# Decode products in the banks of o, their turns two parts later, and the last normaliser stored as rows

## The chip, the core and the metric

The kernel runs on one core of a Trainium2 chip. A core has one TensorE (PE in the profile; its weight loads are PEld), VectorE (DVE), ScalarE (ACT), GpSimd (POOL) and SyncE (SP), each with an instruction stream of its own; they meet at semaphores. Transfers are issued by SP, GpSimd or ScalarE and carried by 16 DMA engines. TensorE writes its results to PSUM, which has 8 banks of 128 x 512 numbers in fp32. The metric is the device time in microseconds (us) of one execution, median over several.

## The reference

One inference step of a decoder trunk of one layer, for a new sequence of 1024 tokens and for 8 sequences with one new (decode) token each, all in fp32, width 1024:

```python
def hybrid_layer(x, h0, conv0, C0, n0, m0, ...):
    hn = rmsnorm(x, g_norm)
    u = hn @ w_in                                   # 1024 -> 7176
    xa, za, uq, uk, uv, uo, zb, ui, uf = jnp.split(u, SPLIT_IDX, axis=-1)
    yA, hA, bufA = rglru_branch(xa, conv0, h0, ...) # conv of 4, gates in 16 blocks, h = a*h + u
    q, k, v = ...                                   # 4 heads of 256
    hB, C, n, m = mlstm_seq(q, k, v, ig, lf, C0, n0, m0)   # 8 chunks of 128 tokens
    yB = ...                                        # sigmoid(uo) * hB, normalised per head
    merged = jnp.concatenate([yA * silu(za), yB * silu(zb)], axis=-1)
    x = x + merged @ w_out                          # 2048 -> 1024
    return x, hA, bufA, C, n, m

def mlstm_chunk(carry, inp):
    ...
    C_new = carry_scale[..., None, None] * C + jnp.einsum('bhs,bshk,bshv->bhkv', decay, k, v)
    n_new = carry_scale[..., None] * n + jnp.einsum('bhs,bshk->bhk', decay, k)
```

The outputs are both y, and the last states of both kinds of sequences; among them is the normaliser p_n of the long sequence, 4 heads of 256 numbers.

## The kernel before

**Products.** A product of fp32 matrices is three matmuls on split operands (`mm3`, L66 to L68): each operand is rounded to a shorter type (hi, a ScalarE cast, L72) and the rest is kept as a second operand (lo, a VectorE subtraction, L73). The input projection is cut into 14 units, counted from 0 (`UNITS`: "v0v1", "x0y0", "q0k0" and so on); a unit is 512 columns of `w_in`, two groups of 256. Each unit is computed by seven block products in place of eight (Q_P1, Q_P2, Q_P5, Q_P6, Q_P7, Q_P3, Q_P4, in this order), with combinations of the weight blocks that VectorE makes (L282, L284 and L290, 128x1024 each). `product` runs a block product in two halves; a half is called a part, some 3 us of TensorE, and after each part the main loop calls `pop_bg`, which puts steps of the other stages (gates, scans, decode, the mLSTM states) between the parts.

**PSUM banks.** They are handed out by tag: o has 3 banks, kv has 2, and tr, s and qp have one each. A product's X (Q_P1, Q_P6, Q_P7, Q_P4) is in kv and its Y (Q_P2 of its own; Q_P5 and then Q_P3 on top of it) in o: four o banks per unit, given out in turn. ScalarE or VectorE reads each bank out (`evac`), and its next user waits for that reader.

**The decode burst.** The 8 decode tokens need the same weights, before VectorE combines them. So `prep(u, Q_P5)`, which makes the operands two products ahead and so runs just before `product(u, Q_P1)`, first calls `dec_unit(u)`: eight matmuls into four groups of rows of one bank tr (L256, 16 rows in the trace since each fp32 matmul counts twice), a ScalarE copy of it to Z (L259), and `turn()`: four transposes of Z (L264) into a bank tr and two VectorE reduces (L267) that add the four groups and write them to the decode operands (dqk, dxz, do, dz). `turn` is put on the list `late`, which the next `pop_bg` runs first: one part later, after the first half of Q_P1. The one bank tr is also used by the RG-LRU gates (L824, every second half) and, in later stages, by `m_b` and the decode outputs.

**The end.** The mLSTM stage goes over 8 chunks and 4 heads (`m_a` to `m_z`). In the last chunk `m_b` stores each head's matrix state (L1260) and its normaliser, which lies as a column 256 of the state with one number per partition (L1261: four stores of 128x2x1 on GpSimd's queue). After that come the last chunk's outputs (`m_n`, `m_zg`, `m_z`), the output projection of the last two tiles (`out_part`, then `last_tile` in three column ranges) and the final norm. Staging tiles (`sg`, tag stg) come from 7 buffers that are given out in turn.

**Order.** The program is built in the order in which the functions are called; from that order, and from which banks and buffers are free, the scheduler of the framework fixes each engine's instruction stream when the program is built. An engine works through its stream in order.

Of the kernel before, what the change touches and what calls it, by code (L numbers as in the profile page):

```python
# [9 lines left out]
F32 = mybir.dt.float32  # L10
# [7 lines left out]
P = 128  # L18
T = 1024
HT = 512  # L20
NB = 8
KC = 8
NH = 4
# [28 lines left out]
def hymba_kernel(  # L52
# [7 lines left out]
    V, A, G, TE = nc.vector, nc.scalar, nc.gpsimd, nc.tensor  # L60
    ld = nc.sync.dma_start
    stq = nc.gpsimd.dma_start

    def mm3(out, ah, al, bh, bl, first, last):

        TE.matmul(out, ah, bh, start=first, stop=False, skip_group_check=True)  # L66
        TE.matmul(out, ah, bl, start=False, stop=False, skip_group_check=True)  # L67
        TE.matmul(out, al, bh, start=False, stop=last, skip_group_check=True)  # L68

    def split(hi, lo, src):  # L70

        a = A.copy(hi, src)  # L72
        V.tensor_tensor(lo, src, hi.bitcast(F32), op=ALU.subtract)  # L73
        return a
# [7 lines left out]
    def ps(tag, shape):  # L82
        return psp.tile(shape, F32, tag=tag, name=f"ps_{tag}", bufs=NBUF.get(tag, 1))

    def const(shape, name, dt=F32):
        return cpool.tile(shape, dt, tag=name, name=name)
# [14 lines left out]
    def sg(shape, name, dt=F32):  # L101

        return stg.tile(shape, dt, tag="stg", name=name)
# [9 lines left out]
    idF = const([P, P], "idF")  # L113
# [77 lines left out]
    def rsqrt_log(out, v, t):  # L191

        A.activation(t, v, AF.Ln, scale=2.0 ** 32)
        A.activation(out, t, AF.Exp, scale=-0.5)
        if len(v.shape) == 2 and v.shape[1] == 1:
            V.scalar_tensor_tensor(t, out, out, v, op0=ALU.mult, op1=ALU.mult)
        else:
            V.tensor_tensor(t, out, out, op=ALU.mult)
            V.tensor_tensor(t, t, v, op=ALU.mult)
        V.tensor_scalar(t, t, -0.25 * 2.0 ** 32, 0.75, op0=ALU.mult, op1=ALU.add)  # L200
        V.scalar_tensor_tensor(out, out, 2.0 ** 16, t, op0=ALU.mult, op1=ALU.mult)
# [18 lines left out]
    late = []  # L220
# [29 lines left out]

    def dec_unit(u):

        pz = ps("tr", [P, 512])
        for k in range(KC):
            g = k % 4
            TE.matmul(pz[32 * g:32 * g + 32, :], hnd[:, NB * k:NB * k + 32], raws[u, k // 4][:, k % 4, :], start=k < 4, stop=k >= 4,  # L256
                      skip_group_check=True)
        Z = sg([P, 512], "Z")
        A.copy(Z, pz)  # L259

        def turn():
            pt = ps("tr", [P, 4, P])
            for m in range(4):
                TE.transpose(pt[:, m, :], Z[:, m * P:(m + 1) * P], idF)  # L264
            for a, (kind, j) in enumerate(units[u]):
                src = pt[:, 2 * a:2 * a + 2].rearrange("p m (g b) -> p m b g", g=4)[:, :, 0:NB, :]
                V.tensor_reduce(dec_dst[kind](j), src, axis=mybir.AxisListType.X, op=ALU.add)  # L267
                if kind == "k":
                    V.tensor_scalar(dec_dst[kind](j), dec_dst[kind](j), 1.0 / 16.0, None, op0=ALU.mult)
        late.append(turn)  # L270


    wops = {}
# [307 lines left out]
    V.tensor_tensor(gd, pgd[0:NB], bgate[0:NB], op=ALU.add)  # L581
    ld(d_gd, gd)
    dec_unit(0)
    load_raw(1, 0)
    load_raw(1, 1)
# [514 lines left out]
    mx = {}  # L1100
# [109 lines left out]
    def m_kv(n, tags):  # L1210

        d, kvs = it[n], []
        for kb, tag in enumerate(tags):
            kv = ps(tag, [P, 258])
            mm3(kv, d["kh"][:, kb * P:(kb + 1) * P], d["kl"][:, kb * P:(kb + 1) * P], *mx["v"], True, True)
            kvs.append(kv)
        return kvs
# [26 lines left out]
    def m_b(n):  # L1244
        c, h = n // 4, n % 4
        d = it[n]
        qc = ps("qp", [P, 258])
        for kb in range(2):
            mm3(qc, d["qh"][:, kb, :], d["ql"][:, kb, :], d["Ch"][:, kb, :], d["Cl"][:, kb, :], kb == 0, kb == 1)
        d["hh"] = hh = mx["p"].tile([P, 257], F32, tag="hh", name="hh", bufs=5)  # L1250
        A.mul(hh, qc[:, 0:257], gi_t[:, c, h:h + 1])
        kvs = m_kv(n, ("kv", "kv"))
        pv = ps("tr", [P, 258])
        mm3(pv, d["ph"], d["pl"], *mx["v"], True, True)
        for kb in range(2):
            V.scalar_tensor_tensor(mx["Cf"][h][:, kb, :], mx["Cf"][h][:, kb, :], cs_b[:, c, h:h + 1], kvs[kb],
                                   op0=ALU.mult, op1=ALU.add)
        V.tensor_tensor(hh, pv[:, 0:257], hh, op=ALU.add)
        if c == NCH - 1:
            stq(p_C[0, 0, h].rearrange("(kb p) v -> p kb v", p=P), mx["Cf"][h][:, :, 0:256])  # L1260
            stq(p_n[0, 0, h].rearrange("(kb p o) -> p kb o", p=P, o=1), mx["Cf"][h][:, :, 256:257])  # L1261

    def m_g(n):

# [22 lines left out]
    def m_zg(c):  # L1287

        x = ch[c]
        for h in range(NH):  # L1290
            A.mul(x["g"][h], x["g"][h], x["m"][:, 3, h:h + 1])

    def m_z(c, pair):

        x = ch[c]
        ht = ps(("s", "qp")[pair], [P, 4, P])
        for i in range(2):
            g = x["g"][2 * pair + i]
            for vb in range(2):
                TE.transpose(ht[:, 2 * i + vb, :], g[:, vb * P:(vb + 1) * P], idF)  # L1300
        s = slice(4 * pair, 4 * pair + 4)
        z = zt[c][:, s, :]
        V.tensor_tensor(z, ht, z, op=ALU.mult)
        if c < NZ:
            stq(d_mz[c][pair], z)
            return
        if pair == 0:
            m_ops(c)
        split(x["mh"][:, s, :], x["ml"][:, s, :], z)

    def m_ops(c):

        ch[c]["mh"], ch[c]["ml"] = ws([P, 8, P], f"mh{c}"), ws([P, 8, P], f"ml{c}")
# [269 lines left out]

    LP = [slice(0, 512), slice(512, 768), slice(768, 1024)]

    def last_tile():
        ms = mx["p2"].tile([P, 6], F32, tag="ms7", name="ms7")
        y = [sg([P, HT], f"y{n}") for n in range(2)]
        yg = [sg([P, HT], f"yg{n}") for n in range(2)]
        for n in range(2):  # L1590
            ld(y[n], d_p[NCH - 1][n])
        mh, ml = ch[NCH - 1]["mh"], ch[NCH - 1]["ml"]
        for i, cs in enumerate(LP):
            p = ps("o", [P, 512])[:, 0:cs.stop - cs.start]
            for k in range(8):
                w = wo[8 + k]
                mm3(p, mh[:, k, :], ml[:, k, :], w[:, 0, cs], w[:, 1, cs], k == 0, k == 7)
            v = (y[0], y[1][:, 0:256], y[1][:, 256:512])[i]
            vg = (yg[0], yg[1][:, 0:256], yg[1][:, 256:512])[i]
            gv = (mx["gf"][0], mx["gf"][1][:, 0:256], mx["gf"][1][:, 256:512])[i]  # L1600
            V.tensor_tensor(v, v, p, op=ALU.add)
            A.activation(p, v, AF.Square, accum_out=ms[:, i:i + 1])
            V.tensor_tensor(vg, v, gv, op=ALU.mult)
            if i == 1:
                V.tensor_scalar(ms[:, 0:1], ms[:, 0:1], ms[:, 1:2], T * EPS, op0=ALU.add, op1=ALU.add)
        V.tensor_scalar(ms[:, 0:1], ms[:, 0:1], ms[:, 2:3], 0.25 / T, op0=ALU.add, op1=ALU.mult)
        rsqrt_log(ms[:, 4:5], ms[:, 0:1], ms[:, 5:6])
        V.tensor_scalar(yg[0], yg[0], ms[:, 4:5], None, op0=ALU.mult)
        A.mul(yg[1], yg[1], ms[:, 4:5])
        for n in range(2):  # L1610
            ld(y_p[0, (NCH - 1) * P:T, n * HT:(n + 1) * HT], yg[n])
# [3 lines left out]
    def fill(k):  # L1615
        for _ in range(k):
            while work:
                if next(work[0], work) is work:
                    work.popleft()
                else:  # L1620
                    break
# [90 lines left out]
    for n in range(4, N):  # L1712
        c, h = n // 4, n % 4
# [13 lines left out]
        if h == 0:  # L1727
            m_n(c - 1)
            fill(2 if n < N2 else 1)
            m_k(n + 1)  # L1730
            fill(1)
            m_b(n)
            fill(1)
        elif h == 1:
# [25 lines left out]
    m_n(last)  # L1760
    fill(3)
    m_zg(last)
    m_z(last, 0)
    fill(1)
    m_z(last, 1)
    while work:
        fill(1)
    tail()
    last_tile()
    es_m.close()  # L1770

# [32 lines left out]
```

## Time and profile before

| | |
|---|---|
| median of 3 runs | 918.35 us (917.04 to 923.15) |
| the profiled execution | 919.27 us, of it 917.2 in the span of the profile |
| TensorE (PE) busy | 902.7 us, 98% of the span |
| its weight loads (PEld) | 749.1 us, 82% |
| VectorE (DVE) | 740.8 us, 81% |
| ScalarE (ACT) | 590.1 us, 64% |
| GpSimd (POOL) | 195.5 us, 21% |
| mean DMA rate | 183 GB/s |

Busy time adds up the instructions of an engine, register and DMA-issuing instructions left out. A row of a timeline gives start (us from the span's start), duration, engine, operation, line, out<-in, sizes, and in brackets how long the engine had stood before it and what released it. The projection units run from about 80 to 625 us, the mLSTM stage to about 890 us, and the rest is the end.

### The profile page before, as it was taken

To read this page: it belongs to the slowest core of one execution; us is meant where nothing else is said; L and a number is where in the kernel's file an instruction comes from. 1 tells how busy PE (TensorE), PEld (TensorE's weight loads), DVE (VectorE), ACT (ScalarE), POOL (GpSimd) and SP (SyncE) were. 2 spreads that over 40 slices of the span, in tenths; PEclk is the share of its full clock that TensorE was granted. 3 is DMA by queue.
4 is the path that set the end of the run, shared out by engine and by line. 5 is a ranking of instruction groups with operands and counts; after the bars stand their busy time and mean duration, and the time that the engine had idled before them with its cause. 6 is when DMAs were issued, how large, how long until landed. Compare 5 with 4: busy or idle time off the path is not lost.

```text
span 917.2 us, 15521 instructions
## 1 busy us (share of the span) xinstructions
PE 902.7 (98%) x5257; PEld 749.1 (82%) x5257; DVE 740.8 (81%) x1532; ACT 590.1 (64%) x1085; POOL 195.5 (21%) x321
## 2 busy tenths in 40 slices
PE   8999999999999999999999999999999999999996
PEld 6897777877777988787779898877778888888886
DVE  6874778978698978789978876679998779889873
ACT  7663456867567676576758686446786568566642
POOL 1111113112312232324332434010111110121120
PEclk9999999999999999999999999999999999999999
DMA  6611457365646566647665747345679889856653
GB/s 201 193 62 45 138 173 243 132 197 188 220 132 208 172 196 205 202 144 256 199 211 193 275 138 243 101 138 185 194 226 280 198 204 302 228 135 182 186 102 88
DMA packets 130584, 167.68 MB, mean 183 GB/s; under 512 B 17700, under 2 KB 98660, under 8 KB 130498
## 3 DMA queue, kind: packets, MB, share of 16 engines
q1 hardware_dynamic: 108790, 103.68, 37.7%
q0 software_dynamic: 21712, 63.02, 21.4%
q8 instruction: 41, 0.67, 0.3%
q14 instruction: 37, 0.30, 0.1%
q10 hardware_dynamic: 4, 0.00, 0.0%
HBM read 108.00 MB, written 62.92 MB: 186 GB/s over the span
## 4 chain that ended last, share of the span: by engine, by line
PE 88%; DVE 4%; ACT 4%; DMA 3%; issue 1%; POOL 0%; ACTq 0%; DVEq 0%; POOLq 0%
PE ps_o L66 14%; PE ps_o L68 14%; PE ps_o L67 14%; PE ps_kv L66 10%; PE ps_kv L67 10%; PE ps_kv L68 10%; PE ps_tr L256 3%; PE ps_s L1195 1%; DMA Cb<-in_state_mlstm_C_dram 1%; DMA W<-d_alpha 1%; PE ps_qp L1013 1%; PE ps_qp L67 1%; PE ps_s L824 1%; PE ps_tr L264 1%; PE ps_qp L68 1%
## 5 line engine op out<-in xcount | busy, mean ns | idle before, releaser
L72 ACT CAST wh<-raw 128x1024 fp32r<-128x1024 f32 x91 | 95.3, 1048 | 73.8 <-PE ps_o L67 24.2
L73 DVE TENSOR_TENSOR wl<-raw,wh 128x1024 fp32r<-128x1024 f32 x91 | 111.0, 1220 | 34.3 <-ACT wh L72 18.8
L66 PE MATMUL ps_kv<-cb_hi,wh 128*128 128x512 f32 x320 | 127.5, 398 | 0.0
L68 PE MATMUL ps_kv<-cb_hi,wl 128*128 128x512 f32 x320 | 125.3, 392 | 0.0
L67 PE MATMUL ps_kv<-cb_lo,wh 128*128 128x512 f32 x320 | 125.2, 391 | 0.0
L66 PE MATMUL ps_o<-cb_hi,wh 128*128 128x512 f32 x240 | 94.7, 395 | 0.0
L68 PE MATMUL ps_o<-cb_hi,wl 128*128 128x512 f32 x240 | 93.7, 390 | 0.0
L67 PE MATMUL ps_o<-cb_lo,wh 128*128 128x512 f32 x240 | 93.5, 390 | 0.0
L66 PEld LDWEIGHTS ps_kv<-cb_hi,wh 128*128 128x128 f32 x320 | 60.1, 188 | 21.3 <-issue 5.5
L67 PEld LDWEIGHTS ps_kv<-cb_lo,wh 128*128 128x128 f32 x320 | 60.2, 188 | 13.4 <-issue 1.7
L68 PEld LDWEIGHTS ps_kv<-cb_hi,wl 128*128 128x128 f32 x320 | 60.1, 188 | 12.9
L66 PE MATMUL ps_kv<-wh,cb_hi 128*128 128x256 f32 x192 | 55.2, 287 | 0.0
L67 PE MATMUL ps_kv<-wl,cb_hi 128*128 128x256 f32 x192 | 54.4, 283 | 0.0
L68 PE MATMUL ps_kv<-wh,cb_lo 128*128 128x256 f32 x192 | 54.3, 283 | 0.0
L66 PEld LDWEIGHTS ps_o<-cb_hi,wh 128*128 128x128 f32 x240 | 45.1, 188 | 10.2 <-issue 0.8
L66 PE MATMUL ps_o<-wo,mh 128*128 128x512 f32 (+1 forms) x136 | 53.1, 390 | 0.0
L68 PEld LDWEIGHTS ps_o<-cb_hi,wl 128*128 128x128 f32 x240 | 45.0, 188 | 9.8
L67 PEld LDWEIGHTS ps_o<-cb_lo,wh 128*128 128x128 f32 x240 | 45.1, 188 | 9.1
L68 PE MATMUL ps_o<-wo,ml 128*128 128x512 f32 (+1 forms) x136 | 51.7, 380 | 0.0
L67 PE MATMUL ps_o<-wo,mh 128*128 128x512 f32 (+1 forms) x136 | 51.5, 379 | 0.0
L66 PE MATMUL ps_o<-wh,cb_hi 128*128 128x256 f32 x144 | 40.9, 284 | 0.0
L67 PE MATMUL ps_o<-wl,cb_hi 128*128 128x256 f32 x144 | 40.7, 283 | 0.0
(547 smaller groups left out, 2600.7 us busy)
## 6 DMA issues: line engine op xcount, KB each, us to landing
raw<-in_w_in_dram SPq DMA_DIRECT2D x55, 512.0 KB
Cb<-in_state_mlstm_C_dram SPq DMA_DIRECT2D x32, 256.0 KB
out_dram<-Cb POOLq DMA_DIRECT2D x32, 256.0 KB, 4.4
qk<-d_qk SPq DMA_DIRECT2D x32, 256.0 KB
ring<-d_ro SPq DMA_DIRECT2D x28, 256.0 KB
d_qk<-s POOLq DMA_DIRECT2D x24, 256.0 KB, 4.5
d_x<-s POOLq DMA_DIRECT2D x16, 256.0 KB, 3.1
zsr<-d_y SPq DMA_DIRECT2D x16, 256.0 KB
```

Of the source, the lines that this page charges most:

```text
L66: TE.matmul(out, ah, bh, start=first, stop=False, skip_group_check=True)
L67: TE.matmul(out, ah, bl, start=False, stop=False, skip_group_check=True)
L68: TE.matmul(out, al, bh, start=False, stop=last, skip_group_check=True)
L72: a = A.copy(hi, src)
L73: V.tensor_tensor(lo, src, hi.bitcast(F32), op=ALU.subtract)
L256: TE.matmul(pz[32 * g:32 * g + 32, :], hnd[:, NB * k:NB * k + 32], raws[u, k // 4][:, k % 4, :], start=k < 4, stop=k >= 4, skip_group_chec ...
L264: TE.transpose(pt[:, m, :], Z[:, m * P:(m + 1) * P], idF)
L824: TE.matmul(pg, w[:, n, :], st["xx"][n], start=k == 0, stop=k == 1)
L1013: TE.matmul(pq[32 * g:32 * g + n, 0:256], q, ds_["C", h * NB + bb][:, kb, :], start=b == 1, stop=b == NB - 1, skip_group_check=True)
L1195: TE.matmul(S, qk[:, 2 + kb, :], qk[:, kb, :], start=kb == 0, stop=kb == 1)
```

## The change

Two things are changed. From unit 2 on a burst takes one of the three o banks, its turn writes into the same bank, and the turn is run one part later than before (after the second half of Q_P1: `late.append(turn)` happens when the first entry is run). At the end the four stores of the normaliser are replaced: GpSimd copies each head's two columns into one tile `ncol`, a matmul with the identity turns it into 8 rows in a kv bank, ScalarE copies these to a staging tile, and one store writes them.

```diff
--- before.py
+++ after.py
@@ -250,7 +250,7 @@
 
     def dec_unit(u):
 
-        pz = ps("tr", [P, 512])
+        pz = ps("tr" if u < 2 else "o", [P, 512])
         for k in range(KC):
             g = k % 4
             TE.matmul(pz[32 * g:32 * g + 32, :], hnd[:, NB * k:NB * k + 32], raws[u, k // 4][:, k % 4, :], start=k < 4, stop=k >= 4,
@@ -259,7 +259,7 @@
         A.copy(Z, pz)
 
         def turn():
-            pt = ps("tr", [P, 4, P])
+            pt = ps("tr", [P, 4, P]) if u < 2 else pz.rearrange("p (m q) -> p m q", m=4)
             for m in range(4):
                 TE.transpose(pt[:, m, :], Z[:, m * P:(m + 1) * P], idF)
             for a, (kind, j) in enumerate(units[u]):
@@ -267,7 +267,7 @@
                 V.tensor_reduce(dec_dst[kind](j), src, axis=mybir.AxisListType.X, op=ALU.add)
                 if kind == "k":
                     V.tensor_scalar(dec_dst[kind](j), dec_dst[kind](j), 1.0 / 16.0, None, op0=ALU.mult)
-        late.append(turn)
+        late.append(turn if u < 2 else lambda: late.append(turn))
 
 
     wops = {}
@@ -1258,7 +1258,9 @@
         V.tensor_tensor(hh, pv[:, 0:257], hh, op=ALU.add)
         if c == NCH - 1:
             stq(p_C[0, 0, h].rearrange("(kb p) v -> p kb v", p=P), mx["Cf"][h][:, :, 0:256])
-            stq(p_n[0, 0, h].rearrange("(kb p o) -> p kb o", p=P, o=1), mx["Cf"][h][:, :, 256:257])
+            if h == 0:
+                mx["n"] = mx["p2"].tile([P, NH, 2], F32, tag="ncol", name="ncol")
+            G.tensor_copy(mx["n"][:, h, :], mx["Cf"][h][:, :, 256])
 
     def m_g(n):
 
@@ -1582,6 +1584,17 @@
 
 
     LP = [slice(0, 512), slice(512, 768), slice(768, 1024)]
+
+    def n_turn():
+
+        mx["pn"] = pn = ps("kv", [P, 512])[0:2 * NH, 0:P]
+        TE.matmul(pn, mx["n"].rearrange("p h k -> p (h k)"), idF, start=True, stop=True)
+
+    def n_out():
+
+        rows = sg([P, HT], "nrows")[0:2 * NH, 0:P]
+        A.copy(rows, mx["pn"])
+        stq(p_n[0, 0].rearrange("h (kb p) -> (h kb) p", p=P), rows)
 
     def last_tile():
         ms = mx["p2"].tile([P, 6], F32, tag="ms7", name="ms7")
@@ -1760,9 +1773,11 @@
     m_n(last)
     fill(3)
     m_zg(last)
+    n_turn()
     m_z(last, 0)
     fill(1)
     m_z(last, 1)
+    n_out()
     while work:
         fill(1)
     tail()
```

Lines up to 1259 keep their numbers; the final norm's lines are 2 to 15 higher. What the scheduler makes of it shows in three places.

TensorE around the burst of unit 5 ("x2y2"; L824 are the gate products, L256 the burst, L264 the turn, L66 to L68 the parts). Before:

```order
L824 MATMUL ps_tr<-xl,ghi 128x512
L824 MATMUL ps_tr<-xl,glo 128x512
L66 MATMUL ps_kv<-cb_hi_187,wh_0_2520 128x512
L67 MATMUL ps_kv<-cb_lo_188,wh_0_2520 128x512
L68 MATMUL ps_kv<-cb_hi_187,wl_0_2521 128x512
```

and a few rows on

```order
L256 MATMUL ps_tr<-raw_5_2352,hnd 32x512 x4
L256 MATMUL ps_tr<-raw_5_2475,hnd 32x512 x4
L67 MATMUL ps_kv<-cb_lo_188,wh_0_2520 128x512
L68 MATMUL ps_kv<-cb_hi_187,wl_0_2521 128x512
L66 MATMUL ps_kv<-cb_hi_187,wh_0_2520 128x512
L67 MATMUL ps_kv<-cb_lo_188,wh_0_2520 128x512
L68 MATMUL ps_kv<-cb_hi_187,wl_0_2521 128x512
L1024 MATMUL ps_qp<-selq,qC 128x8 x2
L264 MATMUL ps_tr<-idF,Z 128x128 x4
```

In the changed kernel:

```order
L824 MATMUL ps_tr<-xl,ghi 128x512
L824 MATMUL ps_tr<-xl,glo 128x512
L256 MATMUL ps_o<-raw_5_2349,hnd 32x512 x4
L256 MATMUL ps_o<-raw_5_2472,hnd 32x512 x4
L66 MATMUL ps_kv<-cb_hi_187,wh_0_2517 128x512
L67 MATMUL ps_kv<-cb_lo_188,wh_0_2517 128x512
L68 MATMUL ps_kv<-cb_hi_187,wl_0_2518 128x512
```

The burst stood inside the first half of Q_P1 and stands ahead of it now, right behind the gates; the turn moves behind the rest of Q_P1, to just before the first matmul of Q_P2.

VectorE in unit 11 (L282, L284 and L290 are the weight combinations, L267 the reduces of the turn, L851 to L879 a step of the RG-LRU). Before:

```order
L282 TENSOR_TENSOR raw_11_5008<-raw_11_5008,raw_11_5193 128x4x256
L851 SCALAR_TENSOR_TENSOR na<-rg,ig 128x512
L267 TENSOR_REDUCE do<-ps_tr 128x16
L852 COPY OC<-na 128x1
L267 TENSOR_REDUCE do<-ps_tr 128x16
L869 SCALAR_TENSOR_TENSOR rm<-na,zsr 128x512
L73 TENSOR_TENSOR wl_2_5441<-raw_11_5008,wh_2_5440 128x1024
L876 TENSOR_TENSOR rt<-rm,r_5418 128x256
L877 TENSOR_TENSOR rt<-r_5418 128x256
L284 TENSOR_TENSOR raw_11_5008<-raw_11_5193,raw_11_5008 128x4x256
L878 TENSOR_TENSOR r_5418<-rm,rt 128x256
```

In the changed kernel:

```order
L869 SCALAR_TENSOR_TENSOR rm<-na,zsr 128x512
L73 TENSOR_TENSOR wl_2_5432<-raw_11_4999,wh_2_5431 128x1024
L876 TENSOR_TENSOR rt<-rm,r_5409 128x256
L877 TENSOR_TENSOR rt<-r_5409 128x256
L284 TENSOR_TENSOR raw_11_4999<-raw_11_5184,raw_11_4999 128x4x256
L878 TENSOR_TENSOR r_5409<-rm,rt 128x256
L267 TENSOR_REDUCE do<-ps_o 128x16
L879 TENSOR_TENSOR r_5409<-rm,r_5409 128x256
L267 TENSOR_REDUCE do<-ps_o 128x16
L290 TENSOR_TENSOR raw_11_4999<-raw_11_5184,raw_11_4999 128x4x256
L73 TENSOR_TENSOR wl_3_5525<-raw_11_4999,wh_3_5524 128x1024
```

The two reduces went from ahead of L73 and L284 to behind L284, one step ahead of L290; in units 3, 6, 7, 9, 12 and 13 they stand behind L290.

GpSimd at the end (L1260 stores the matrix state, L1261 the normaliser, L1531 rows of y). Before:

```order
L1260 DMA out_dram<-Cf_5974 128x2x256
L1261 DMA out_dram<-Cf_5974 128x2x1
L1260 DMA out_dram<-Cf_5975 128x2x256
L1261 DMA out_dram<-Cf_5975 128x2x1
L1531 DMA out_dram<-y_9781 128x512
L1531 DMA out_dram<-y_9782 128x512
L1531 DMA out_dram<-y_9981 128x512
```

In the changed kernel (L1533 is the old L1531):

```order
L1260 DMA out_dram<-Cf_5964 128x2x256
L1263 COPY ncol<-Cf_5964 128x2
L1260 DMA out_dram<-Cf_5965 128x2x256
L1263 COPY ncol<-Cf_5965 128x2
L1533 DMA out_dram<-y_9770 128x512
L1533 DMA out_dram<-y_9771 128x512
L1597 DMA out_dram<-nrows 8x128
L1533 DMA out_dram<-y_9970 128x512
```

Each store of columns became a copy, and one store of rows is queued between the y stores. On TensorE the one new matmul (L1591) stands between the last product of the tile before (L68 into o) and the transposes of the last head (L1302, before L1300).

## The prediction

> **What bounds the kernel now.** I read the page first, then the table of stretches, then TensorE's waits, then the timeline around each wait.
>
> ```profile
> span 917.2 us, 15521 instructions
> PE 902.7 (98%) x5257; PEld 749.1 (82%) x5257; DVE 740.8 (81%) x1532; ACT 590.1 (64%) x1085; POOL 195.5 (21%) x321
> PEclk9999999999999999999999999999999999999999
> PE 88%; DVE 4%; ACT 4%; DMA 3%; issue 1%; POOL 0%; ACTq 0%; DVEq 0%; POOLq 0%
> ...
> core 0: us, PE busy (x) PEld busy (x) DVE busy (x) ACT busy (x) POOL busy (x), PEclk, DMA share, GB/s
> 80.00:625.00 545.00, 542.26 (x3105) 444.28 (x3104) 436.16 (x776) 353.59 (x524) 138.41 (x222) 1.00 0.57 183
> 890.00:917.20 27.20, 20.29 (x115) 17.17 (x113) 12.73 (x32) 7.71 (x22) 2.20 (x4) 0.93 0.41 88
> ...
> 910.01 0.28 PE L68 MATMUL ps_o<-wo,ml 128*128 128x256 f32 x1
> ```
>
> TensorE sets the time: 88% of the chain that ended last, at a clock of 9 tenths or more in every slice. In the stretch of the projection units (80 to 625 us), where the first half of the change acts, it idles 545.00 - 542.26 = 2.74 us in all. So a change that only takes waits off TensorE there has at most about that to win. In the last 27.2 us, where the second half acts, the table shows 27.20 - 20.29 = 6.91 us without it, and the last matmul ends at 910.29, 6.91 us before the end: TensorE has no gap there before its last matmul.
>
> Who ends those waits between 80 and 890 us (engine, line, releaser: us in total, times, longest):
>
> ```profile
> PE ps_tr L256 <- ACT ig L774: 2.0, 1, 2.0
> PE ps_kv L66 <- ACT kh L1203: 0.6, 1, 0.6
> PE ps_tr L264 <- ACT Z L259: 0.5, 2, 0.3
> PE ps_o L66 <- ACT ro L72: 0.5, 1, 0.5
> PE ps_s L659 <- DVE gx L629: 0.2, 1, 0.2
> ```
>
> The first and third rows are the decode burst (L256) and its turn (L264), which the change touches; the other three (L1203, L72, L629) it doesn't.
>
> **Term 1: the burst leaves the bank of the gates.** In unit 5 the RG-LRU gate product (L824) fills the one bank tr, and the burst wants the same bank:
>
> ```profile
> 247.81 0.39 PE L824 MATMUL ps_tr<-xl,glo 128*128 128x512 f32 x1
> 249.42 0.40 PE L66 MATMUL ps_kv<-cb_hi,wh 128*128 128x512 f32 x1
> 251.86 1.92 PE L256 MATMUL ps_tr<-raw,hnd 128*32 128x512 f32 x16 [2.05 <-ACT ig L774]
> ...
> 249.06 0.72 ACT L992 ACTIVATE Cb<-Cb,dGI 128x512 f32<-128x512 f32 x1 [2.61 <-DMA Cb<-in_state_mlstm_C_dram]
> 249.81 0.58 ACT L355 COPY c<-ps_kv 128x512 f32<-128x512 f32 x1
> 251.13 0.68 ACT L774 ACTIVATE ig<-ps_tr,hb 64x512 f32<-64x512 f32 x1
> 254.00 0.59 ACT L259 COPY Z<-ps_tr 128x512 f32<-128x512 f32 x1
> ```
>
> ScalarE stands at L992 for a state transfer until 249.06, reads the gate out of tr until 251.81, and TensorE idles 2.05 us. After the change the burst writes an o bank. Three o banks go round; a unit takes five turns of them instead of four, and the burst's bank was last used by the second half of product Q_P2 of the unit before, read out many parts earlier. So the wait has no reason left: -2.05 us. The other eleven bursts of the changed units show no such wait and give nothing. What is late next: ScalarE is as late as before, so its next debts matter. The kv bank that it still owes is copied out by 250.39 (L355), while TensorE would then be in the burst (1.92 us) and has a whole part of the other kv bank ahead of it; I count no new wait.
>
> **Term 2: the turn waits for its copy.** Twice the turn came before ScalarE had copied the burst out:
>
> ```profile
> 208.49 0.57 ACT L259 COPY Z<-ps_tr 128x512 f32<-128x512 f32 x1
> 209.12 0.66 PE L264 MATMUL ps_tr<-idF,Z 128*128 128x128 f32 x4 [0.28 <-ACT Z L259]
> 477.24 0.59 ACT L259 COPY Z<-ps_tr 128x512 f32<-128x512 f32 x1
> 477.88 0.65 PE L264 MATMUL ps_tr<-idF,Z 128*128 128x128 f32 x4 [0.25 <-ACT Z L259]
> ```
>
> One part later (a part is a product's half, about 3 us) both copies are done: -0.28 - 0.25 = -0.53 us. The number of matmuls, copies and reduces stays, so moving them adds nothing by itself.
>
> **Term 3: the new wait.** The bank of the burst goes next to the first half of Q_P5, so that matmul now waits until VectorE has reduced the turn (L267) out of it. Behind it stands all of TensorE. The reduces moved on VectorE too: in the new order they stand beside or behind the combinations L284 and L290 of the weights. How early those are done in the present trace bounds the wait; the tightest unit (11) and a loose one (12):
>
> ```profile
> 531.20 1.22 DVE L284 TENSOR_TENSOR raw<-raw,raw 128x1024 f32<-128x1024 f32 x1
> 532.67 1.22 DVE L290 TENSOR_TENSOR raw<-raw,raw 128x1024 f32<-128x1024 f32 x1
> 534.72 0.28 PE L66 MATMUL ps_o<-wh,cb_hi 128*128 128x256 f32 x1
> ...
> 575.63 1.23 DVE L290 TENSOR_TENSOR raw<-raw,raw 128x1024 f32<-128x1024 f32 x1
> 582.83 0.47 PE L66 MATMUL ps_o<-cb_hi,wh 128*128 128x512 f32 x1
> ```
>
> L290 ends 534.72 - 533.89 = 0.83 us before Q_P5's first matmul in unit 11 and 582.83 - 576.86 = 5.97 us before it in unit 12. Two reduces take some 0.4 us. So with VectorE where it is now the wait is 0 in all units, in the tightest by less than half a microsecond. Lower end 0; the upper end is in the second rival.
>
> By the Trainium skill ("PSUM — Partial Sum Buffer", section "PSUM bank collisions raise a hardware error") two engines may not be in one bank and quadrant at once, whatever columns they touch, so sharing a bank ties burst, turn and product to each other whole. The 2.05 us above agree with it: the burst waited for the last reader of the whole bank. By that rule every user that is added to the ring of o is a new place to wait, which is the second rival.
>
> **Term 4: the normaliser as rows.** Gone are four stores of 128x2x1 (L1261); new are four GpSimd copies, one matmul, one ScalarE copy of 8x128 and one store.
>
> ```profile
> 112.02 0.39 PE L66 MATMUL ps_kv<-cb_hi,wh 128*128 128x512 f32 x1
> 112.25 0.39 PE L67 MATMUL ps_kv<-cb_lo,wh 128*128 128x512 f32 x1
> 112.61 0.20 PE L671 MATMUL ps_qp<-ends,hsel 32*4 32x16 f32 x2
> 112.74 0.50 PE L68 MATMUL ps_kv<-cb_hi,wl 128*128 128x512 f32 x1
> 890.95 0.83 PE L1300 MATMUL ps_s<-idF,hh 128*128 128x128 f32 x4
> 73.12 0.21 POOL L609 COPY igc<-gs 128x32 f32<-128x32 f32 x1
> 886.69 0.70 POOL L1261 DMA_DIRECT2D out_dram<-Cf  x1
> 892.74 0.62 ACT L72 CAST mh<-z 128x512 fp32r<-128x512 f32 x1 [0.65 <-DVE z L1303]
> DMA to landing us min/median/max: 9.0/11.3/15.6
> 899.56 0.69 DVE L1577 TENSOR_TENSOR y<-y,ps_o 128x512 f32<-128x512 f32 x1 [3.08 <-DMA y<-d_p]
> 907.25 0.28 PE L66 MATMUL ps_o<-wo,mh 128*128 128x256 f32 x1
> ```
>
> - The matmul is on TensorE's path. A small fp32 one between two large ones put 0.49 us between their starts (112.25 to 112.74) where 0.23 is usual (112.02 to 112.25): +0.26. Bounds: 0, if it fits into the wait ahead of L1300, and 0.83, the whole of L1300's row. It is nearest to L671; I take 0.26.
> - The last GpSimd copy takes the place of the last L1261 at 886.7, at 0.21 us by L609; the matmul stands ahead of L1300 at 890.95, some 4 us later. Nothing waits: 0. If that cover were gone, z would wait, and the copy would cost its 0.21.
> - ScalarE's copy stands ahead of L72 at 892.74, where it idles 0.65 us; the row of 128x512 takes 0.62, so 8x128 fits: 0. The new store goes to POOL's queue behind it, ahead of the last two y stores, whose y isn't added up before 899.56.
> - The four stores took 9.0 to 15.6 us to land for 1 KB each (the landing row above is L1261's). In one queue with the y stores, they can be what delays the load on which VectorE waits 3.08 us at 899.56. That wait is hidden: its bank is wanted again only by the last third of the last tile, at 907.25. Bounds of this gain: 0 and 3.08; I take 0.
>
> The Trainium skill ("DMA: Bandwidth & Descriptors", section "Rules for kernel authors") says that a transfer whose last dimension isn't contiguous goes out as one descriptor per element, and to rearrange it. The landing times agree. By that rule alone the tail would gain up to the 3.08 us; that is the third rival.
>
> **The sum.** -2.05 - 0.53 + 0 + 0.26 + 0 = -2.32 us. The profiled execution took 919.27 us (span 917.2 and 2.07 around it): 916.95. It is 0.92 above the median 918.35 of the runs shown, which gives 916.03. Whether the late state transfer of unit 5 was in the other runs isn't known, so I forecast between the two: **916.5 us**, own range 914.5 to 918.
>
> **Rivals.**
> 1. *The wait moves, it doesn't go.* ScalarE stays as late for the state transfer of unit 5 as it is, and the order of ScalarE, VectorE and SP is a new one: a kv or o bank is evacuated late instead. For it: the 2.61 us in which ScalarE stood at L992, with its copies queued behind. Against: only 2.74 us of TensorE idle in 545 us, so the banks mostly absorb this. Terms 1 and 2 come to 0, term 4 stays: 918.35 + 0.26, **918.6 us**.
> 2. *The shared bank (slower).* Q_P5 waits for L267. The slacks of the 12 changed units lie between 0.83 and 5.97; spread evenly and with VectorE later by d, the mean loss of a unit is (d - 0.83)^2 / (2 x 5.14). It decides from d = 0.83 on. For d = 3 it is 0.46 us, 12 units 5.5 us: **922.0 us**; for d = 4, 0.98 us and 11.7 us: 928.2. For it: VectorE is 81% busy and the reduces were put later. Against: L267 itself is short, and the new rows put it before L290 in the tight unit 11.
> 3. *The tail gains too.* If the last loads set the end through a bank, the 3.08 us come on top: 916.5 - 3.1 = **913.4 us**. Against: TensorE has no gap before 910.29, so nothing earlier sets the end.
>
> **How the numbers follow.** Forecast 0.55, rival 1 0.22, rival 2 0.16, rival 3 0.07. The runs before lie between 917.04 and 923.15, so 1% (9.2 us) is about what a measurement of this kernel can tell from no change. Faster by more would need 909.2: below what TensorE's idle time leaves; 0.03 for what I overlooked. Slower by more needs 927.5, the end of rival 2: 0.07. Within 1%: 0.90. The range takes in rival 3 below and rival 1 with rival 2's first half above: 912.8 to 922.5.
>
> **What would show it.** In the profile after: no row of L256 with a wait for L774 and no row of L264 waiting for L259; TensorE's idle between 80 and 625 us near 0.2 us instead of 2.74; Q_P5's first matmul, after the burst, without a wait for L267; the small matmul before the last transposes within 0.3 us; the last y load issued earlier than now. Wrong would be: waits of L66 on o for L267 in several units (rival 2), waits of L66 on kv or o for ScalarE's copies at the places of the state transfers (rival 1), or an end that came earlier with unchanged TensorE idle (rival 3).

## The result, and the profile after

The changed kernel takes 916.28 us in the median of 21 runs (915.53 to 917.62). The kernel before, run beside it 21 times, took 919.81 us (917.04 to 923.35). The ratio is 0.9962, with a 95% interval of 0.9954 to 0.9971. So 3.5 us are gone in the median, and the spread shrank from 6.3 to 2.1 us. The profiled execution took 916.28 us, of it 914.2 in the span. Its page, and the table of stretches (us, then busy time and count of PE, PEld, DVE, ACT and POOL, TensorE's granted clock, DMA share, GB/s):

```profile
span 914.2 us, 15522 instructions
PE 902.0 (99%) x5259; PEld 748.8 (82%) x5259; DVE 741.2 (81%) x1532; ACT 590.1 (65%) x1086; POOL 194.2 (21%) x322
...
80.00:625.00 545.00, 544.75 (x3118) 446.50 (x3117) 439.34 (x788) 353.76 (x525) 138.24 (x222) 1.00 0.57 185
890.00:914.20 24.20, 17.25 (x101) 15.14 (x99) 10.11 (x24) 5.49 (x17) 1.10 (x2) 0.90 0.22 74
```

In the projection units TensorE now idles 545.00 - 544.75 = 0.25 us instead of 2.74. Of its waits between 80 and 890 us one row is left, and it is none that the change touches:

```profile
PE ps_o L66 <- ACT ro L72: 1.1, 1, 1.1
```

How far ahead this puts TensorE shows at the first matmul of Q_P2 in unit 13 (before, then changed), and at the last matmul of all (changed; before it stood at 910.01):

```profile
622.87 0.39 PE L66 MATMUL ps_o<-cb_hi,wh 128*128 128x512 f32 x1
619.95 0.48 PE L66 MATMUL ps_o<-cb_hi,wh 128*128 128x512 f32 x1
...
906.97 0.28 PE L68 MATMUL ps_o<-wo,ml 128*128 128x256 f32 x1
```

So 622.87 - 619.95 = 2.92 us of the 910.01 - 906.97 = 3.04 us between these two executions are gained by the last of the units. Behind the last matmul the end is as it was: 24.20 - 17.25 = 6.95 us without TensorE, 6.91 before. Unit 5 again, first TensorE, then ScalarE:

```profile
247.58 1.92 PE L256 MATMUL ps_o<-raw,hnd 128*32 128x512 f32 x16
255.52 0.60 PE L264 MATMUL ps_o<-idF,Z 128*128 128x128 f32 x4
...
249.25 0.72 ACT L992 ACTIVATE Cb<-Cb,dGI 128x512 f32<-128x512 f32 x1 [3.35 <-DMA Cb<-in_state_mlstm_C_dram]
251.32 0.69 ACT L774 ACTIVATE ig<-ps_tr,hb 64x512 f32<-64x512 f32 x1
252.88 0.59 ACT L259 COPY Z<-ps_o 128x512 f32<-128x512 f32 x1
```

ScalarE stood for the state transfer even longer than before (3.35 us, 2.61 then), and read the gate out of tr until 252.01. TensorE didn't wait for it: the burst had begun at 247.58, and the turn came at 255.52, 2.05 us after Z was written (253.47).

The shared bank, in unit 11, the tightest one (VectorE's second reduce and its reading of Q_P2's first half, L333, then the first matmul of Q_P5), and the end (TensorE around the new matmul, in the changed kernel and then in the one before):

```profile
530.15 0.21 DVE L267 TENSOR_REDUCE do<-ps_o 128x16 f32<-128x64 f32 x1
532.55 0.67 DVE L333 TENSOR_TENSOR s<-s,ps_o 128x512 f32<-128x512 f32 x1
531.92 0.28 PE L66 MATMUL ps_o<-wh,cb_hi 128*128 128x256 f32 x1
...
887.48 0.39 PE L68 MATMUL ps_o<-wo,ml 128*128 128x512 f32 x1
887.79 0.39 PE L1591 MATMUL ps_kv<-idF,ncol 128*8 128x128 f32 x2
888.11 0.66 PE L1302 MATMUL ps_s<-idF,hh 128*128 128x128 f32 x4
888.52 0.47 PE L66 MATMUL ps_o<-wo,mh 128*128 128x512 f32 x1
```

```profile
890.57 0.39 PE L68 MATMUL ps_o<-wo,ml 128*128 128x512 f32 x1
891.54 0.47 PE L66 MATMUL ps_o<-wo,mh 128*128 128x512 f32 x1
```

The reduces are done at 530.36, 1.56 us before Q_P5 starts, and no row of L66 waits for them. Q_P2's first half is read out only behind that start, from 532.55 on, and its second half later still. So of the three o banks Q_P5 can only have taken the burst's, as the prediction said. From the L68 ahead of the transposes to the L66 behind them it is 888.52 - 887.48 = 1.04 us with the new matmul and 891.54 - 890.57 = 0.97 without: it costs 0.07.

One thing that the prediction had priced at nothing changed by much: how long the stores and loads around the last chunk take. From issue to landing of the four stores of the matrix state (256 KB each, L1260), in the changed kernel and then in the one before; and VectorE's last use of so, the output gate that SP loads (L1275 is the old L1273), in the same order:

```profile
DMA to landing us min/median/max: 2.5/2.8/3.3
...
883.04 0.42 DVE L1275 SCALAR_TENSOR_TENSOR hh<-so,hh 128x256 f32<-128x256 f32 x1
```

```profile
DMA to landing us min/median/max: 3.8/11.2/15.3
...
887.03 0.42 DVE L1273 SCALAR_TENSOR_TENSOR hh<-so,hh 128x256 f32<-128x256 f32 x1 [0.82 <-DMA so<-d_so]
```

With the four 1 KB stores of columns between them, the large stores took four times as long, and the last load of so came 0.82 us late. In this execution that cost nothing. The experiments show what it costs in others.

### The profile page after: what moved, and what is told of

Its sections match the earlier page's. It is cut to its first block, busy times and chain, and to the rows that moved or that the text cites. A ratio compares the mean times of both kernels' runs of the same rounds, so it can differ in the third digit from the quotient of the medians.

```text
span 914.2 us, 15522 instructions
## 1 busy us (share of the span) xinstructions
PE 902.0 (99%) x5259; PEld 748.8 (82%) x5259; DVE 741.2 (81%) x1532; ACT 590.1 (65%) x1086; POOL 194.2 (21%) x322
## 2 busy tenths in 40 slices
DMA packets 130488, 167.68 MB, mean 183 GB/s; under 512 B 17596, under 2 KB 98564, under 8 KB 130402
## 4 chain that ended last, share of the span: by engine, by line
PE 93%; DVE 2%; ACT 2%; DMA 1%; issue 1%; POOL 0%; ACTq 0%; DVEq 0%; POOLq 0%
PE ps_o L66 15%; PE ps_o L68 15%; PE ps_o L67 14%; PE ps_kv L66 11%; PE ps_kv L68 11%; PE ps_kv L67 11%; PE ps_o L256 2%; PE ps_s L1195 1%; PE ps_qp L1013 1%; PE ps_s L824 1%; PE ps_tr L824 1%; PE ps_qp L67 1%; PE ps_qp L66 1%; PE ps_qp L68 1%; PE ps_s L1197 1%
## 5 line engine op out<-in xcount | busy, mean ns | idle before, releaser
L72 ACT CAST wh<-raw 128x1024 fp32r<-128x1024 f32 x91 | 95.4, 1048 | 75.8 <-PE ps_o L67 23.2
L73 DVE TENSOR_TENSOR wl<-raw,wh 128x1024 fp32r<-128x1024 f32 x91 | 110.9, 1219 | 32.5 <-ACT wh L72 17.5
L66 PE MATMUL ps_kv<-cb_hi,wh 128*128 128x512 f32 x320 | 127.3, 398 | 0.0
L68 PE MATMUL ps_kv<-cb_hi,wl 128*128 128x512 f32 x320 | 125.3, 392 | 0.0
L66 PE MATMUL ps_o<-cb_hi,wh 128*128 128x512 f32 x240 | 95.2, 397 | 0.0
L68 PE MATMUL ps_o<-cb_hi,wl 128*128 128x512 f32 x240 | 93.7, 390 | 0.0
L66 PEld LDWEIGHTS ps_kv<-cb_hi,wh 128*128 128x128 f32 x320 | 60.1, 188 | 22.3 <-issue 5.5
L68 PEld LDWEIGHTS ps_kv<-cb_hi,wl 128*128 128x128 f32 x320 | 60.1, 188 | 12.9
L66 PE MATMUL ps_kv<-wh,cb_hi 128*128 128x256 f32 x192 | 55.1, 287 | 0.0
L68 PE MATMUL ps_kv<-wh,cb_lo 128*128 128x256 f32 x192 | 54.3, 283 | 0.0
L68 PEld LDWEIGHTS ps_o<-cb_hi,wl 128*128 128x128 f32 x240 | 45.0, 188 | 9.8
L66 PE MATMUL ps_o<-wo,mh 128*128 128x512 f32 (+1 forms) x136 | 53.0, 390 | 0.0
L66 PEld LDWEIGHTS ps_o<-cb_hi,wh 128*128 128x128 f32 x240 | 45.1, 188 | 9.7 <-issue 0.8
L68 PE MATMUL ps_o<-wo,ml 128*128 128x512 f32 (+1 forms) x136 | 51.6, 380 | 0.0
L66 PE MATMUL ps_o<-wh,cb_hi 128*128 128x256 f32 x144 | 41.0, 284 | 0.0
```

## The experiments

The change has three parts: the bank (burst and turn in an o bank), the delay (the turn one part later) and the rows (the normaliser). All eight combinations were run, in medians of 12 runs (before: four groups of 18 to 35 runs, medians 919.27 to 919.81; the change: 21; delay and rows: 11, without one run of 3149.91 us). Each was run beside one of the groups of before, but not beside the others; the ratios below are to that group and go by means, not medians.

| parts | median us | lowest | highest |
|---|---|---|---|
| none (before) | 919.5 | 917.0 | 926.8 |
| bank (e1_bank) | 919.16 | 916.06 | 926.07 |
| delay (e2_delay) | 919.20 | 917.81 | 922.23 |
| rows (e3_rows) | 919.31 | 917.86 | 920.22 |
| bank, delay (e4_decode) | 919.23 | 915.71 | 925.24 |
| bank, rows (f1_bank_rows) | 918.12 | 916.25 | 921.39 |
| delay, rows (f2_delay_rows) | 919.28 | 918.35 | 921.67 |
| all (the change) | 916.28 | 915.53 | 917.62 |

No part alone moves the median by more than 0.4 us, and all together move it by 3.2 to 3.5.

**The first four: each part alone.** The bank alone:

```diff
-        pz = ps("tr", [P, 512])
+        pz = ps("tr" if u < 2 else "o", [P, 512])
...
-            pt = ps("tr", [P, 4, P])
+            pt = ps("tr", [P, 4, P]) if u < 2 else pz.rearrange("p (m q) -> p m q", m=4)
```

> The bank alone: from unit 2 on the burst and its turn take an o bank, the turn stays one part behind, the normaliser is stored as before. Theory A (the gain is the burst's wait for the gate in unit 5): the wait of 2.05 us for L774 is gone, the turns of units 4 and 10 may still wait 0.3 us each for Z, so 2.0 to 2.5 us faster than before in a profiled run, and more than half of the 3.5 us that lie between the medians of before and of the change. Rival B (the gain sits in the stores of the normaliser): within 0.5 us of before. Rival C (the delay of the turn is needed for it): slower than A says, with waits of L264 for Z in several units, and less than 1 us faster.

Measured: 919.16 (916.06 to 926.07), ratio to before 1.0012 (0.9990 to 1.0034). The profiled run, 916.98 us, fits theory A, but the median doesn't: 4 of 12 runs took 922 to 926. By its number alone the median fits B and C; the profile has the sign of C, in two units. The burst doesn't wait any more, and the turn does, where ScalarE is late:

```profile
209.00 0.66 PE L264 MATMUL ps_o<-idF,Z 128*128 128x128 f32 x4 [0.48 <-ACT Z L259]
476.34 0.65 PE L264 MATMUL ps_o<-idF,Z 128*128 128x128 f32 x4 [1.07 <-ACT Z L259]
```

The delay alone (`late.append(turn if u < 2 else lambda: late.append(turn))`, all else as before):

> The delay alone: turns one part later, burst and turn in bank tr as before, normaliser as before. Theory A: the two waits of L264 for Z are gone (0.53 us, with the restart of TensorE after each at most 0.9), the wait of L256 for L774 stays at about 2 us; 0.3 to 0.9 us faster, if the later turn does not hold tr against the gates, 0 to 1 us slower if it does. Rival C: 2 to 3.5 us faster.

Measured: 919.20 (917.81 to 922.23), ratio 1.0004 (0.9990 to 1.0018). In the profile the waits for Z are gone, the wait of L256 for L774 is 1.5 us, and there is a new one, since the later turn holds tr against the gates:

```profile
303.01 0.47 PE L824 MATMUL ps_tr<-xl,ghi 128*128 128x512 f32 x1 [0.58 <-DVE dqk L267]
```

The median lies 0.3 us under before's, between the two branches of theory A, and both of their signs stand in the profile.

The rows alone (the last three hunks of the change's diff, without the first three):

> The normaliser's rows alone, bursts and turns as before. Theory A: nothing or +0.26 us, so -0.3 to +0.5 us against before; the y load of the last tile but one is not waited for any more (3.08 us of VectorE) and the end does not move by it. Rival B: 1.5 to 3.5 us faster.

Measured: 919.31 (917.86 to 920.22), ratio 0.9996 (0.9986 to 1.0007): the median as expected. What I hadn't expected is the missing upper end: no run above 920.3. The profiled run (920.19 us) loses its time in the units: nobody waits for so, but TensorE idles 545.00 - 541.27 = 3.73 us between 80 and 625 us, 1.6 us of it for the gate in unit 5 and 1.9 for Z.

Unit 5 alone in the o bank (both conditions `u != 5` instead of `u < 2`):

> Only the burst and the turn of unit 5 take an o bank; all other units, the delay and the normaliser are as before. Theory A in its narrow form (one wait, in one unit): 2.0 to 2.5 us faster in a profiled run, and the times of the runs scatter as little as those of the change (915.5 to 917.6) instead of before's 917.0 to 923.4, since it is the late state transfer of that place that varies. Rival D (the state transfers come late at other places in other runs, so several bursts pay): about 2 us faster in the median, but with the scatter of before.

Measured: 918.78 (916.33 to 925.79), ratio 1.0005 (0.9985 to 1.0025). Not theory A: two runs took 925.7. Nor is the median 2 us lower, as D said. After these four, what made some runs 6 to 10 us longer was open; the runs with the bank above 922 had a mean clock of 0.994 to 0.996, most others 0.997 to 0.999.

**The next four: where the long runs lose their time.** Bank and delay, columns as before (the first three hunks of the diff):

> The bank and the delay together, the normaliser stored as columns as before. Theory E (bank and delay belong together: a late ScalarE holds up the burst through the gate's bank, or, with the bank alone, the turn through Z; only both together let it be late unnoticed): the whole change's time, 915.5 to 917.6, median 916.0 to 916.8, no run above 919. Rival F (the stores of columns are what makes the runs with the bank alone scatter): median near 919 with runs above 922, as with the bank alone.

Measured: 919.23 (915.71 to 925.24), ratio 0.9989 (0.9963 to 1.0014). Theory E falls as far as the long runs go, and the profile caught one of them (span 922.8). VectorE, ScalarE, TensorE, and the stretches behind:

```profile
891.00 0.42 DVE L1273 SCALAR_TENSOR_TENSOR hh<-so,hh 128x256 f32<-128x256 f32 x1 [5.92 <-DMA so<-d_so]
894.36 1.71 ACT L1291 ACTIVATE hh<-hh,ms 128x256 f32<-128x256 f32 x4 [0.36 <-DVE ms L201]
894.92 1.12 PE L1300 MATMUL ps_s<-idF,hh 128*128 128x128 f32 x4 [5.09 <-ACT hh L1291]
895.69 0.78 PE L66 MATMUL ps_o<-wo,mh 128*128 128x512 f32 x1
896.26 0.63 PE L67 MATMUL ps_o<-wo,mh 128*128 128x512 f32 x1
...
80.00:625.00 545.00, 544.85 (x3120) 446.90 (x3119) 439.99 (x791) 354.16 (x525) 138.25 (x223) 1.00 0.57 185
893.00:896.00 3.00, 1.08 (x5) 0.97 (x6) 2.69 (x11) 2.43 (x9) 0.29 (x1) 0.50 0.51 130
896.00:900.00 4.00, 4.00 (x16) 3.14 (x15) 2.13 (x5) 1.33 (x4) 0.82 (x2) 0.65 0.48 177
...
DMA to landing us min/median/max: 9.9/11.9/14.1
```

Read upwards from TensorE's L1300: TensorE stood 5.09 us for hh, which ScalarE scales (L1291) once VectorE has all four heads, and VectorE stood 5.92 us for the last load of so. That load was issued at 875.23, between the second and the third store of columns; the last row is the landing of the large stores beside it. After the stall TensorE was granted half its clock for a few us (0.50 and 0.65 in the two stretches). In the units (80 to 625 us) TensorE idled 0.15 us: there bank and delay do all that they do in the change.

The bank alone, two more single executions of the same kernel:

> One more look at the bank alone, whose 12 runs lay between 916.06 and 926.07. Theory E: waits of L264 for Z (ScalarE behind L992), in unit 5 or 10, together as long as the run is above some 915.5 us, if the run is a long one; about 0.5 to 1.6 us of them if it is a short one. Rival F: no such waits, the time is lost behind 625 us.

> The same kernel, a third look, with the same expectations as the second: the length of the waits of L264 for Z says how long the run is (E), or the loss lies behind 625 us (F).

The first of them was a long one, 931.02 us, the second a short one, 918.03 us. The long one:

```profile
895.61 0.43 DVE L1273 SCALAR_TENSOR_TENSOR hh<-so,hh 128x256 f32<-128x256 f32 x1 [7.58 <-DMA so<-d_so]
899.52 0.69 PE L1300 MATMUL ps_s<-idF,hh 128*128 128x128 f32 x2 [6.75 <-ACT hh L1291]
```

Its waits of L264 for Z come to 1.5 us, and those of the short run to 1.9. So the long runs lose most at the end, as rival F said, and the turns cost 1.5 to 1.9 us in long and short runs alike.

Not all of it is lost there. Without its stall the long run of bank and delay would have started the last transposes at 894.92 - 5.09 = 889.83, where the change starts them at 888.11: it was already 1.72 us behind. The stall adds 5.09, and by the last matmul (915.58 against 906.97) the low clock another 1.80. Of what it lost earlier, the most shows at TensorE's wait for ro (L72) near 675 us, some 190 us ahead of the first store of columns. It is longer in the two long runs than in any other trace (1.92 and 1.79 us; 0.4 to 1.2 in the others), and in both TensorE runs at half its pace behind it.

State scaling on GpSimd, with the bank alone (`G.tensor_scalar(C, C, dGI[:, b, h:h + 1], None, op0=ALU.mult)` for `A.mul(C, C, dGI[:, b, h:h + 1])`):

> The bank alone, and the multiplication of the decode states (L992) on GpSimd instead of ScalarE, so that ScalarE no longer stands for a state transfer. Theory E: with its cause gone, neither the burst nor the turn waits, the delay isn't needed: median 915.5 to 917.5 and no run above 919, unless GpSimd, which now stands for the transfers with the stores of the products queued behind, holds up a staging tile (then a new wait on ScalarE's or VectorE's evacuations shows and the time is 1 to 5 us above). Rival F: scatter up to 926 as with the bank alone.

Measured: 928.23 in 7 runs (926.25 to 936.10), ratio 1.0097 (1.0061 to 1.0133). That is some 11 us above the 915.5 to 917.5 of theory E, more than the 1 to 5 us allowed for a held-up GpSimd. It tells nothing of theory E, since a new bound hides it: GpSimd stands 7 us for a transfer, VectorE's next step on that state stands with it, and ScalarE and TensorE follow:

```profile
469.82 3.11 POOL L992 TENSOR_SCALAR Cb<-Cb,dGI 128x512 f32<-128x512 f32 x2 [6.99 <-DMA Cb<-in_state_mlstm_C_dram]
476.70 0.63 ACT L846 ACTIVATE na<-na 128x512 f32<-128x512 f32 x1 [6.66 <-DVE na L845]
478.00 0.58 PE L66 MATMUL ps_kv<-wh,cb_hi 128*128 128x256 f32 x1 [3.50 <-ACT c L355]
```

**The last four: the parts without the columns.** Bank and rows (the change with `late.append(turn)`):

> The bank and the rows, without the delay. Theory G (the stores of columns clog the transfers at the end in some runs, so that the last load of the output gate comes late and TensorE stands 5 to 7 us; bank and delay act in the middle only): no run above 919, no wait of VectorE for so at L1273, and against the change only the turns of some units wait for Z, 0.5 to 1.9 us in all: median 916.8 to 918.2. Theory E (bank and delay only work together): median near 919 and runs above 921.

Measured: 918.12 (916.25 to 921.39), ratio to before 0.9983 (0.9966 to 0.9999). As theory G says, in the median; two runs of 12 (919.14 and 921.39) are longer than it allows.

Delay and rows (the change with burst and turn in tr):

> The delay and the rows, burst and turn in bank tr as before. Theory G: the wait of the burst for the gate in unit 5 stays (1.5 to 2 us), the turns don't wait for Z; between the rows alone (919.3) and the change (916.3): median 917.5 to 919, no run above 920.5.

Measured: 919.28 (918.35 to 921.67), above what was expected. In its profile the burst of unit 5 waits 1.65 us for the gate, and the gate of unit 6 waits 0.75 us for the reduces (L824 for L267), as with the delay alone. Three runs above 921 remain here without any column store, so not every long run comes from the stores.

Bank and delay without any store of p_n:

> Bank and delay, and the last normaliser is not stored at all (this leaves out the output p_n). Theory G: with no stores of columns the runs above 918 are gone, as with the rows: median 915.7 to 916.6, and the difference to the change is the price of the rows, 0 to 0.5 us. Rival F2 (the rows help by something else, an extra staging buffer in the ring or the order of the engines): scatter to 920 and more as with the columns.

Measured: 915.78 (914.93 to 918.88), ratio 0.9958 (0.9941 to 0.9975). With the columns taken away and nothing put in their place the long runs go (one of 12 is 918.88). So it is the stores of columns, not the extra buffer that the rows take. The traces say the same: VectorE waits for the last load of so in all eight executions of kernels that store columns (0.19 to 7.58 us), and in none of the six of kernels that don't. Against this kernel the change is 0.5 us slower in the median: the price of the rows, at most, since the two weren't run side by side.

The turn of units 2 to 11 two more parts later:

> The change with the turn of units 2 to 11 two parts later still, so that it stands just ahead of the first matmul of Q_P5. By the second rival of the prediction (the shared bank makes Q_P5 wait for the reduces): in these 10 units Q_P5 waits for the transposes, the two reduces and what VectorE does between, 1.1 to 3.5 us each, so 11 to 35 us slower than the change. If the shared bank were harmless whatever the delay: within 1 us of the change.

Measured: 919.53 in 10 runs (917.64 to 921.17), 3.3 us above the change's median: neither 11 to 35 nor within 1. Unit 8, where the turn now stands right ahead of Q_P5, and the one place that waits long (unit 2):

```profile
399.19 0.60 PE L264 MATMUL ps_o<-idF,Z 128*128 128x128 f32 x4
399.55 0.48 PE L66 MATMUL ps_o<-cb_hi,wh 128*128 128x512 f32 x1
401.92 0.34 DVE L267 TENSOR_REDUCE dxz<-ps_o 128x16 f32<-128x64 f32 x2
...
132.16 0.76 PE L66 MATMUL ps_o<-cb_hi,wh 128*128 128x512 f32 x1 [2.27 <-DVE s L333]
132.72 0.63 PE L67 MATMUL ps_o<-cb_lo,wh 128*128 128x512 f32 x1
125.00:135.00 10.00, 7.73 (x31) 6.15 (x30) 7.49 (x13) 5.04 (x8) 1.13 (x2) 0.86 0.73 221
```

In unit 8 Q_P5 starts 2.4 us before the reduces, so its first half isn't in the burst's bank. In unit 2 it waits for L333, VectorE's reading of Q_P2, and not for L267. So with the turn this late the first half of Q_P5 gets the bank that Q_P2 has left. The burst then only takes one bank out of the ring, and in this trace that cost a long wait in one unit, where VectorE was late with L333.

## Why the prediction was right, and where it wasn't

The time forecast, 916.5 us, lies 0.2 from the median. The step from before is a worse match: 1.85 us forecast from the median shown, 3.2 to 3.5 measured against the medians of later runs. That the time fits so closely is in part luck: the median of three runs from which it was taken lies 0.9 to 1.5 us under those of the later groups, and what the sum lacks is of that size. (Of the two ranges given, the narrow one, 914.5 to 918, held.)

**Terms 1 and 2** (2.58 us together) hold: 2.74 - 0.25 = 2.49 us of idle time are gone in the units, and TensorE is 2.92 us ahead there; the 0.34 us above the forecast weren't traced. What the prediction didn't see is that they aren't two terms. The bank alone brings the burst forward but leaves ScalarE late, and the wait moves to the turn (0.48 and 1.07 us in one run, 1.9 in another); the delay alone keeps 1.5 to 1.65 us of the burst's wait and moves the turn's to the gate (0.58, 0.75). Without columns at the end the medians are 919.31 (neither), 918.12 (bank), 919.28 (delay) and 916.28 (both), in groups that weren't run side by side: the delay is worth 1.8 us with the bank and nothing without it. So rival 1, the wait that moves, is what happens to each half, and the forecast is what happens to both, because the turn's 2.05 us of cover hide a ScalarE that is later than before.

**Term 3** (0) holds in all 12 changed units, with 1.56 us or more between reduces and Q_P5. Rival 2 had the sharing right, but VectorE wasn't late enough for it. Its price stays untested: in f4, which was to show it, the burst's bank isn't the next one of Q_P5. There 10 turns that came two parts later cost 3.3 us, most of it in one unit.

**Term 4**: the matmul's 0.26 measured 0.07. The step that failed is the last bullet, the gain of the stores, taken as 0 from bounds of 0 and 3.08. The prediction looked for the cover in one profiled execution and followed only the load that waited there (y at 899.56), which is hidden indeed: it is not waited for now, and the end did not come earlier for it. The load that counts is another one of the same queue, so, which was 0.82 us late in that execution and harmless, and 5.92 to 7.58 late in the long ones. With bank and delay in place the columns cost 919.23 - 916.28 = 2.95 us in the median, of groups that weren't run side by side. In the two executions compared above next to nothing of this shows (0.12 us behind the units): it is a gain in the median of many runs. Rival 3 had the cause (stores of columns delay loads) with the wrong load and a chance of 0.07.

The Trainium skill ("DMA: Bandwidth & Descriptors", section "Rules for kernel authors") had spoken for this gain, since a store whose last dimension isn't contiguous goes out as one descriptor per element. The landing times agree, 11.2 against 2.8 us for the stores beside it. The packets don't show it: the page of the profile lists 130584 before and 130488 after, 96 fewer, where 4 stores of 256 numbers would be 1024, and in the trace before the four stores are 64 packets of 64 bytes, so 16 numbers each.

**Left open**: why the columns hardly raise the median while the burst still waits (919.5, and 919.31 with the rows alone), and do so by 1.0 us with the bank and 2.95 us with bank and delay. In the two long runs whose trace I have, the loads behind the first large store (qk, vt and the last but one of so) were issued 2.2 and 2.3 us after it, against 0.6 us in most short ones; the delay alone had 1.4, and the rows alone 1.9 without a wait. The last load of so itself was issued 3.7 us behind the second large store in long and short runs alike. Which transfer holds which back was not traced further, and neither was the wait for ro.

## What to carry to other kernels

A wait that is hidden in one profiled execution may still set the median: look at the spread of the runs, and price what is late at its worst, not only where the trace shows it. Edits that each move the median by less than 0.4 us here move it by more than 3 together, so test them together before dropping one. Stores of a few bytes per partition cost more through the transfers beside them than by their own time; turning them on TensorE cost 0.07 us of its path here.

## What the runs showed of the hardware that I had not expected

Stalls of some 2 us can cost TensorE more than their length. After the stalls of 5.09 us (bank and delay) and 2.27 us (f4) matmuls of 512 columns followed at 0.43 to 0.57 us instead of 0.23, and the granted clock was 0.50 and 0.86 in those stretches; a stall of 1.92 us did the same:

```profile
675.74 0.50 PE L66 MATMUL ps_o<-wr4h,ro 128*128 128x512 f32 x1 [1.92 <-ACT ro L72]
675.00:681.00 6.00, 5.26 (x23) 4.49 (x24) 5.28 (x14) 5.28 (x14) 0.55 (x1) 0.72 0.95 283
...
252.00:255.00 3.00, 3.00 (x22) 1.35 (x18) 2.96 (x5) 2.56 (x4) 0.00 (x0) 1.00 0.66 218
```

The last row is the stretch behind the 2.05 us stall of the kernel before: a clock of 1.00. The Trainium skill ("TensorE: Matmul & The Clock Gate", section "HAM oscillation — how this bites in real kernels") puts the limit at gaps of some 3.4 us. The runs here show shorter ones that were followed by the low clock and one that was not. After the stall of 1.92 us the pace was halved for some 3.5 us, so by an estimate from these rows a stall of 2 us can cost 2 us or nearly 4.
